# Decoder layer on one core: every engine of the attention stage in the order of emission, softmax in steps of its own, another beginning and end of the stage

## The chip, the cores and the metric

The kernel runs on one core of a Trainium2 chip. The metric is the device time of one execution in microseconds; the figure for the kernel before is the median of three runs. TensorE (PE) multiplies and transposes; VectorE (DVE), ScalarE (ACT) and GpSimd (POOL) work on tiles; SyncE (SP) issues most DMAs. Each engine takes its instructions in a fixed order.

## The reference

One layer, for a prompt of 1024 tokens and 8 sample sequences of 8 new tokens with 4096 cached positions each (64 columns), 1088 columns in all. Cut to what matters:

```python
h = rms_norm(x, norm1) * (1 + scale1) + shift1
z = h @ w_in     # q, kc, vc, ks, vs, kw, vw, gates, conv (bg, cg, h), pool
k_cmp = rms_norm(compress(full[:, :, 0], ...)); v_cmp = compress(full[:, :, 1], ...)
o_cmp, p_cmp = cmp_attention(q, k_cmp, v_cmp, q_pos)
top_i, sel_ok = select_blocks(p_cmp, ...)            # 16 of the 64-token blocks
o_slc = slc_attention(q, top_i, sel_ok, ...)
o_win = window_attention(...)                        # 512 positions back
o_attn = g[..., 0:1] * o_cmp + g[..., 1:2] * o_slc + g[..., 2:3] * o_win
x = x + gate1 * (concat[o_attn, y_conv, y_pool] @ w_out)
x = x + gate2 * swiglu(rms_norm(x, norm2) * (1 + scale2) + shift2, w_up, w_down)
```

There are 8 query heads and 2 key/value heads of 64. The prompt has 16 blocks of 64 tokens, so the selected branch sees every causal block there; for the samples blocks are chosen. The compression makes one key and value of every 32 positions, stride 16, by a small network over the whole cache.

## The kernel before

**Stages.** Normalisation and the input projection run until about 374 us of the span, attention from there to about 832 us, then the output projection and the SwiGLU network. Data are held with features on partitions.

**Who sets the order.** The class `Kernel` emits instructions from tasks, which are generators with a priority (`spawn`, `run`): a task yields the time from which it can go on, and the run takes the task with the lowest priority number that is ready within `MARGIN` (1.2 us). For that the class keeps a clock per engine, `self.t`, advanced by `use` with a cost for each instruction and by `mm` and `tr` for PE. `hold` keeps a task until a condition is true. The emitted instructions then pass through the framework's scheduler, which orders each engine's instructions by its own model of their time; `issue_after(x)` forces that an instruction stands behind x. `together` uses it so that the matmuls of a group follow each other.

**Prompt attention.** 32 units: 8 blocks of 128 queries (`j`), two halves of the heads (`half`), and for each the selected branch with the compressed one (`slc`) and the window branch (`win`). `scores` (from L1015) treats two head pairs (`hl`): three matmuls for each product, since keys and queries are split in a high and a low part (`kh`, `kl`, `qh`, `ql`), into banks of PSUM; the mask with the running maximum on DVE (L1068) reads a bank and frees it; exp with a sum on ACT (L1080); reciprocal and gate on DVE (L1082, L1086); the scale on POOL (L1090). All that is emitted by `scores` itself, pair after pair, into one tile `P` for four heads and 1024 keys, of which there are two. `values` (from L1095) transposes `P` on PE (L143), evacuates it to `pt` (L161, L163), multiplies with the values and stores to `mix_d` in DRAM.

**Samples.** `sample_select` attends to the compressed keys of two sequences and chooses blocks (`kvc`, `qb`, `kn`); 36 sample units follow, nine for each pair of sequences: scores of cached keys (`unit,qb`), mask on DVE (L1325, L1328), exp on ACT (L1332), transposes of `e`, matmuls with the values (`unit,spt`). After the ninth `sample_combine` (from L1360) forms the weights `cw` on ACT and sums twelve parts with `co` on DVE (L1382), transposes it, copies it to `smo` and stores it to `mix_d`.

**Compression.** `compress` works through octets of pages: 16 matmuls each of a `stream` tile (three buffers) with weights. `gather` loads a tile page by page, six pages from SP and two from POOL (L531).

**The edges.** The projection's tiles end with `q0` to `q3`; `head_norm` (L766, L767) normalises each. Then `key_stacks` and `query_parts` split keys and queries, `constants3` (L289 to L342) and `sample_setup` make what the samples need. At the end `output_projection` loads `w_raw` from SP, splits it in `w_hi` and `w_lo`, loads `mixc` from `mix_d` (L1468: the first half of the columns from SP, the second from ACT) and `x1a` (L1494, from ACT), and multiplies `mh`, the high part of `mixc`.

The waits that gate a unit are these:

```python
yield from self.hold(lambda: self.v_done >= u - 1)                                        # prompt_attention
yield from self.hold(lambda: "at" in st and u in self.loads and self.u_done >= u - 1)     # sample_attention
```

Of the kernel before, what the change touches and what calls it, by code (L numbers as in the profile page):

```python
# [17 lines left out]
P = 128  # L18
D = 1024
KT = D // P  # L20
SEQ = 1024
# [40 lines left out]

class Kernel:
    def __init__(self, ctx, tc, ins, outs):
        self.ctx, self.tc, self.nc, self.i, self.o = ctx, tc, tc.nc, ins, outs
        self.ps_ctx = None
        self.t = {"pe": 0.0, "act": 0.0, "dve": 0.0, "pool": 0.0, "dma": 0.0}
        self.table = None
        self.tasks = []
# [56 lines left out]
    def mm(self, out, lhsT, rhs, start, stop, chain=False):  # L126
# [12 lines left out]
        return self.nc.tensor.matmul(out, lhsT, rhs, start=start, stop=stop, skip_group_check=chain)  # L139

    def tr(self, out, in_, ident=None):
        self.t["pe"] += 0.11 if ident is None else 0.03
        return self.nc.tensor.transpose(out, in_, self.ident if ident is None else ident)  # L143

    def together(self, steps):

        last = steps[0]()
        for f in steps[1:]:
            with self.tc.issue_after(last.ins):
                last = f()  # L150
# [442 lines left out]
    def compress_prompt(self, pool):  # L593
# [19 lines left out]
        for kv in range(2):  # L613
            for k in range(KT):
                self.mm(uv[:, kv, 0:P], self.w1[:, kv * KT + k, :], rv[:, kv, k], k == 0, k == KT - 1)
        r = self.compress_evac(uv[:, :, 0:P], vt, pre, 0, 8)
# [269 lines left out]
    def input_projection(self, h):  # L886
# [12 lines left out]
        order = ["kc", "vc", "cg0", "ch0", "bg0", "cg1", "ch1", "bg1", "p0", "ks", "p1", "kw", "q0", "q1", "q2", "q3"]  # L899
        self.ada2 = self.pool("ada2", "left")  # L900
        self.ada_pool = self.ada2.__enter__()
        with self.pool("z", "left") as z, self.pool("hn") as hn:
# [36 lines left out]
            self.spawn(lambda: 0.9 if self.octets <= PACE * (self.z_steps - z0) else 1.5, self.compress_more())  # L939
            with self.pool("conv") as cv:  # L940
                for j in range(2):
                    st = dict(zip(("cg", "ch", "bg"), self.conv_steps(cv, j)))
                    yield from tiles([n + str(j) for n in ("cg", "ch", "bg")],
                                     lambda nm, ch, acc, c0, n: st[nm[:2]](ch, acc))
# [7 lines left out]
            with self.pool("pre") as pp:  # L952
                self.spawn(0.6, self.up_weights_ahead(pp, 1))
                yield from tiles(["q0", "q1", "q2", "q3"], qk)
                yield from self.hold(lambda: self.formed == 2)
            yield from self.hold(lambda: self.prompt_at and self.heads == 18 and 5 in self.ada_at)
# [30 lines left out]
    def key_stacks(self):  # L987

        nc = self.nc
        for j in range(2):  # L990
            kh, kl = self.K[j]
            for a, n, src in ((64, SEQ, self.ksw[:, j, 0:SEQ]), (0, 64, self.kcp)):
                self.split(kh[:, a:a + n], kl[:, a:a + n], src, n)
                yield max(self.t["dve"], self.t["act"]) - 1.0
        self.stacks_at = max(self.t["dve"], self.t["act"])


    def prompt_attention(self, pool):
# [3 lines left out]
        for u, (j, half, br) in enumerate(units):  # L1002
# [3 lines left out]
            yield from self.hold(lambda: self.v_done >= u - 1)  # L1006
# [8 lines left out]
    def scores(self, pool, u, j, half, br):  # L1015
# [31 lines left out]
        Pt = pool.tile([P, 4, SEQ], F32, name="P", bufs=2)  # L1047
        ready = 0.0
        K = self.K[kj]
        for hl in range(2):  # L1050
            r = 2 * half + hl
            st = pool.tile([P, 2, 2, 4], F32, name="st", bufs=6)
            t = [0.0, 0.0]
            for x, (pieces, parts) in enumerate(banks):
# [9 lines left out]
                for g in range(2):  # L1064
                    t[g] = self.t["pe"] + 0.1
                    for (y, col, p0, n, mk) in parts:
                        z = x if y == 0 else 0
                        nc.vector.tensor_tensor_reduce(out=Pt[:, 2 * g + hl, col:col + n], in0=S[g][:, p0:p0 + n], in1=mk,  # L1068
                                                       scale=-1.0, scalar=3e38, op0=OP.add, op1=OP.min,
                                                       accum_out=st[:, g, y, z:z + 1])  # L1070
                        t[g] = self.use("dve", 0.07 + n * 0.00105, t[g])
# [4 lines left out]
            for y, (b, col, n) in enumerate(seg):  # L1076
                sy = st[:, :, y]
                for g in range(2):
                    Ps = Pt[:, 2 * g + hl, col:col + n]
                    nc.scalar.activation(Ps, Ps, AF.Exp, scale=-1.0, bias=sy[:, g, 0:1], accum_out=sy[:, g, 1:2])  # L1080
# [1190 lines left out]
```

## Time and profile before

| | |
|---|---|
| three runs | 1677.99, 1681.29, 1681.86 us, median 1681.29 us |
| the profiled execution | 1672.63 us, span 1671.0 us, mean granted clock 0.977 |
| instructions | 35661 |
| PE busy in the span | 1562.1 us (93%) |
| DVE, ACT, POOL busy | 1090.4, 779.0, 665.4 us |

Times in the trace are counted from the span's start. A row of a timeline gives start, duration, engine, line, operation, output and inputs, shape, how many such instructions stand together, and in square brackets the engine's idle time before and what released it. Lines are those of the kernel before. A wait belongs to the instruction that waited; one that waits for several things is put down to the one that came last. The profiled execution is 8.7 us shorter than the median of the three others.

### The profile page before, as it was taken

The numbers are of one execution on the slowest core, as the hardware profiler recorded it, in microseconds if no ns is written. First come the engines' busy times: TensorE is split into PE (matmuls) and PEld (weight loads), VectorE is DVE, ScalarE is ACT, GpSimd is POOL, SyncE is SP. The second block draws the span as 40 slices with busy tenths as digits, with TensorE's granted clock in tenths as the row PEclk, the third lists the DMA queues.
The fourth block names the chain that finished last, engine by engine and source line by source line (L and its number), as shares of the span: only waits on it lengthen the run. The fifth ranks groups of instructions, "written<-read, shape, count | busy, mean of one in ns | idle before, by whom it ended". The sixth has DMA issues, their size and how long they took to land. (4 is left out here: it accounts for less than half of the span.)

```text
span 1671.0 us, 35661 instructions
## 1 busy us (share of the span) xinstructions
PE 1562.1 (93%) x12697; PEld 1391.8 (83%) x12697; DVE 1090.4 (65%) x2625; ACT 779.0 (47%) x1829; POOL 665.4 (40%) x789
## 2 busy tenths in 40 slices
PE   6899999997999899899599989999999999899998
PEld 2898997896777566566499989999999999899988
DVE  4723234777555666767579878777777775577695
ACT  3522115335765666666466534433434443344462
POOL 3120110114333123223013356554555455788695
PEclk9999999998999999999899999999999999999999
DMA  9585654425467363245685564446444335966553
GB/s 336 182 287 162 207 168 148 144 95 162 133 186 217 100 193 104 70 131 147 210 303 187 198 221 168 143 145 232 145 145 143 142 136 204 393 234 241 182 168 121
DMA packets 186834, 302.12 MB, mean 181 GB/s; under 512 B 26353, under 2 KB 114994, under 8 KB 186338
## 3 DMA queue, kind: packets, MB, share of 16 engines
q1 hardware_dynamic: 166786, 272.20, 49.1%
q0 software_dynamic: 5856, 16.24, 3.0%
q10 hardware_dynamic: 14016, 11.41, 2.2%
q8 instruction: 101, 1.65, 0.4%
q14 instruction: 75, 0.61, 0.1%
HBM read 233.43 MB, written 70.53 MB: 182 GB/s over the span
## 5 line engine op out<-in xcount | busy, mean ns | idle before, releaser
L139 PE MATMUL bank<-b_hi,w_hi 128*128 128x272 f32 x1232 | 351.8, 291 | 7.3 <-DVE f_g L1631 2.9
L139 PE MATMUL bank<-b_lo,w_hi 128*128 128x272 f32 x1232 | 353.8, 289 | 1.7 <-DVE b_lo L171 1.7
L139 PE MATMUL bank<-b_hi,w_lo 128*128 128x272 f32 x1232 | 348.9, 288 | 0.7 <-DVE w_lo L171 0.7
L139 PEld LDWEIGHTS bank<-b_hi,w_hi 128*128 128x128 f32 x1232 | 231.0, 189 | 10.6 <-ACT b_hi L175 4.7
L139 PEld LDWEIGHTS bank<-b_lo,w_hi 128*128 128x128 f32 x1232 | 232.8, 189 | 2.4 <-DVE b_lo L171 2.3
L139 PEld LDWEIGHTS bank<-b_hi,w_lo 128*128 128x128 f32 x1232 | 231.0, 189 | 0.9 <-DVE w_lo L171 0.9
L1090 POOL TENSOR_SCALAR P<-P,st 128x128 f32<-128x128 f32 (+10 forms) x192 | 109.5, 584 | 230.2 <-DVE st L1086 139.1
L171 POOL TENSOR_TENSOR w_s<-w_raw 128x512 f32<-128x512 f32 (+1 forms) x88 | 126.7, 1440 | 64.6 <-DVE w_lo L171 50.5
L171 DVE TENSOR_TENSOR w_lo<-w_raw,w_hi 128x512 fp32r<-128x512 f32 (+2 forms) x121 | 116.9, 975 | 53.8 <-ACT w_hi L175 50.7
L139 PEld LDWEIGHTS bank<-stream 128*128 128x128 f32 x1056 | 127.4, 198 | 17.9 <-issue 13.0
L175 ACT ACTIVATE w_hi<-w_raw 128x512 fp32r<-128x512 f32 (+2 forms) x122 | 80.9, 678 | 130.1 <-PE bank L139 78.2
L171 POOL TENSOR_TENSOR x<-x,d_m 128x272 f32<-128x272 f32 x144 | 126.6, 901 | 34.9 <-DVE x L1833 20.5
L139 PE MATMUL bank<-stream 128*128 128x128 f32 x1056 | 133.8, 284 | 6.2 <-DMA stream<-in_cacheA 5.7
L1080 ACT ACTIVATE P<-P,st 128x640 f32<-128x640 f32 (+12 forms) x192 | 112.7, 588 | 46.1 <-DVE st L1074 26.6
L139 PE MATMUL bank<-h_hi,w_hi 128*128 128x384 f32 (+1 forms) x384 | 130.1, 339 | 0.9 <-ACT py L879 0.6
L139 PE MATMUL bank<-g,w_hi 128*128 128x272 f32 x616 | 121.5, 293 | 8.3 <-DVE x L1833 6.5
L139 PE MATMUL bank<-h_hi,w_lo 128*128 128x384 f32 (+1 forms) x384 | 126.5, 330 | 0.0
L171 DVE TENSOR_TENSOR w_lo<-w_s,w_hi 128x512 fp32r<-128x512 f32 (+1 forms) x124 | 116.8, 944 | 14.8 <-ACT w_hi L175 12.6
L139 PE MATMUL bank<-h_lo,w_hi 128*128 128x384 f32 (+1 forms) x384 | 125.8, 328 | 0.0
L139 PE MATMUL bank<-g,d_hi 128*128 128x272 f32 x616 | 120.2, 291 | 2.6 <-DVE x L1833 1.7
L1833 DVE SCALAR_TENSOR_TENSOR x<-bank,mod,x 128x272 f32<-128x272 f32 (+1 forms) x192 | 87.3, 476 | 40.8 <-PE bank L139 35.5
L139 PEld LDWEIGHTS bank<-g,w_hi 128*128 128x128 f32 x616 | 98.2, 191 | 10.1 <-DVE x L1833 7.4
(371 smaller groups left out, 3732.3 us busy)
## 6 DMA issues: line engine op xcount, KB each, us to landing
g_d<-f_s SPq DMA_DIRECT2D x57, 544.0 KB, 3.3
g<-g_d SPq DMA_DIRECT2D x56, 544.0 KB, 6.3
wada<-in_wada SPq DMA_DIRECT2D x96, 256.0 KB, 5.4
stream<-in_cacheA SPq DMA_DIRECT2D x192, 128.0 KB, 3.2
w_raw<-in_wup SPq DMA_DIRECT2D x40, 512.0 KB, 4.5
unit<-in_cacheB SPq DMA_DIRECT2D x152, 128.0 KB, 2.4
stream<-in_cacheB SPq DMA_DIRECT2D x104, 128.0 KB, 2.4
w_raw<-in_wout SPq DMA_DIRECT2D x24, 512.0 KB, 4.6
```

The source lines that it names most:

```text
L139: return self.nc.tensor.matmul(out, lhsT, rhs, start=start, stop=stop, skip_group_check=chain)
L171: (self.nc.vector if eng == "dve" else self.nc.gpsimd).tensor_tensor(out, a, b, op=op)
L175: self.nc.scalar.activation(hi, src, AF.Copy)
L1080: nc.scalar.activation(Ps, Ps, AF.Exp, scale=-1.0, bias=sy[:, g, 0:1], accum_out=sy[:, g, 1:2])
L1090: nc.gpsimd.tensor_scalar(Ps, Ps, sy[:, g, 3:4], 0.0, op0=OP.mult, op1=OP.add)
L1833: nc.vector.scalar_tensor_tensor(out[:, :n], acc[:, :n], self.mod[:, 5, m, 0:1], out[:, :n], op0=OP.mult, op1=OP.add)
```

## The change

It touches the attention stage and its two edges. The matmuls of the layer stay the same.

- **Order of emission.** In attention each PE instruction is issued behind the PE instruction emitted before it (`in_turn`), and VectorE, ScalarE and GpSimd are reached through a wrapper, `InTurn`, that does the same for each of them, DMAs issued by ScalarE and GpSimd included. SP is not in turn. `together` only calls its steps. The class's costs are replaced by durations that were measured, and a change between half and full rows of the PE array costs 0.08 us on its clock.
- **Softmax.** `scores` emits matmuls and masks only; the exps are one step of a new task `softmax`, the reciprocals, gates and scales another. The samples' exp is a task too, `sample_exp`.
- **Buffers.** `P` holds two heads and has three buffers; the window branch has its own `Pw`, three of 704 columns. A head pair waits for `v_done >= u - 2 + hl`. A sample unit waits for `u_done >= u - 2`, with three `e` and `spt`.
- **Beginning.** The tiles of the projection come in another order, with `bg1` of the convolution last. One octet more is loaded early. The exp table is loaded after the last square root by a small exp. Keys and queries are split in pieces, what the first unit needs first. `constants3` and `sample_setup` come after the first unit's scores.
- **End.** `sample_combine` starts at the exp of the ninth unit, adds ten terms, and the last one when its part is there. The store of `smo` and the loads of `mixc` and `x1a` for the first half of the columns go from POOL.

```diff
+class InTurn:
+    def __getattr__(self, name):
...
+        def call(*args, **kwargs):
+            with self.tc.issue_after(self.last.ins) if self.last else ExitStack():
+                r = f(*args, **kwargs)
+            if hasattr(r, "ins"):
+                self.last = r
+            return r
...
+    def in_turn(self, half, f):
...
+        last, was = self.turn
+        if half != was:
+            self.t["pe"] += 0.08
+        with self.tc.issue_after(last.ins):
+            last = f()
+        self.turn = last, half
+        return last
...
-        order = ["kc", "vc", "cg0", "ch0", "bg0", "cg1", "ch1", "bg1", "p0", "ks", "p1", "kw", "q0", "q1", "q2", "q3"]
+        order = ["kc", "vc", "cg0", "ch0", "bg0", "p0", "ks", "p1", "kw", "q0", "q1", "cg1", "ch1", "q2", "q3", "bg1"]
...
+    def key_stacks(self, ap):
+        self.key_parts(0, 64, P)
+        self.key_parts(0, 0, 64)
+        self.query_parts(ap, 0)
+        self.key_parts(1, 64, P)
+        for j in range(2):
+            self.key_parts(j, 64 + P, SEQ - P)
+        self.key_parts(1, 0, 64)
...
-            yield from self.hold(lambda: self.v_done >= u - 1)
...
-        Pt = pool.tile([P, 4, SEQ], F32, name="P", bufs=2)
+        slc = br == "slc"
         for hl in range(2):
+            yield from self.hold(lambda: self.v_done >= u - 2 + hl)
+            Pt.append(pool.tile([P, 2, SEQ if slc else 5 * P + 64], F32, name="P" if slc else "Pw", bufs=3))
...
-                        t[g] = self.use("dve", 0.07 + n * 0.00105, t[g])
+                        t[g] = self.use("dve", 0.16 + n * 0.00105, t[g])
...
+            self.spawn(-1, self.softmax(j, r, st, Pt[hl], seg, max(t), done))
...
+    def softmax(self, j, r, st, Ps_, seg, t, done):
+        yield t - MARGIN
...
+                nc.scalar.activation(Ps, Ps, AF.Exp, scale=-1.0, bias=sy[:, g, 0:1], accum_out=sy[:, g, 1:2])
+                ta = self.use("act", 0.28 + n * 0.00084, t + 0.1, table="exp")
+        yield ta + 0.1 - MARGIN
...
+                nc.gpsimd.tensor_scalar(Ps, Ps, sy[:, g, 3:4], 0.0, op0=OP.mult, op1=OP.add)
+                at = self.use("pool", 0.25 + n * 0.00084, td + 0.1)
+        done.append(at + 0.1)
...
-            yield from self.hold(lambda: "at" in st and u in self.loads and self.u_done >= u - 1)
+            yield from self.hold(lambda: "at" in st and u in self.loads and self.u_done >= u - 2)
...
+        if nx == 9:
+            self.spawn(2, self.sample_combine(pool, st, u // 9))
...
-        for c in range(11):
+        for c in (0, 1, 2, 3, 4, 5, 6, 7, 8, 10):
             nc.vector.scalar_tensor_tensor(o, part[:, c], w[:, c:c + 1], o, op0=OP.mult, op1=OP.add)
-        yield self.use("dve", 4.0, self.t["pe"]) + 0.5
+        yield self.use("dve", 3.7, self.t["pe"])
+        yield from self.hold(lambda: "last" in st)
+        nc.vector.scalar_tensor_tensor(o, part[:, 9], w[:, 9:10], o, op0=OP.mult, op1=OP.add)
...
-        nc.sync.dma_start(self.mix_d[:, 0:4, SEQ + 16 * p:SEQ + 16 * p + 16],
-                            mo.rearrange("p r b t -> p r (b t)"))
+        nc.gpsimd.dma_start(self.mix_d[:, 0:4, SEQ + 16 * p:SEQ + 16 * p + 16], mo.rearrange("p r b t -> p r (b t)"))
...
+        with self.tc.issue_after(self.last_sqrt.ins):
+            self.nc.scalar.activation(self.warm, self.eps, AF.Exp)
...
+        yield from self.hold(lambda: self.scored >= 1)
+        self.constants3(ap)
+        self.sample_setup(ap)
...
-                (nc.sync if c == 0 else nc.scalar).dma_start(t, self.mix_d[:, k:k + 2, c * HALF:c * HALF + HALF])
+                (nc.gpsimd if c == 0 else nc.scalar).dma_start(t, self.mix_d[:, k:k + 2, c * HALF:c * HALF + HALF])
...
-                nc.scalar.dma_start(dst, src)
+                (nc.gpsimd if c == 0 else nc.scalar).dma_start(dst, src)
```

Counted in the two orders, PE changes between tile shapes in attention 323 times before and 276 times now, and between half and full rows 233 and 195 times.

In the following rows a name's number tells instances of one tile apart; in the changed kernel the instructions of DVE, ACT and POOL in attention all have the wrapper's line, L78, a matmul has L164 and a transpose L169. The first place is the start of attention on PE, before, from the sums of squares of the last query tiles (`h_sq`) on:

```order
L139 MATMUL bank<-h_sq,mean_h 128x384
L139 MATMUL bank<-h_sq,mean_h 128x320
L139 MATMUL bank<-stream 128x128 x16
L139 MATMUL bank<-kh_3506,qh 128x192 x2
L139 MATMUL bank<-kl_3507,qh 128x192 x2
L139 MATMUL bank<-kh_3506,ql 128x192 x2
...
L139 MATMUL bank<-kh_3508,ql 128x128 x2
L139 MATMUL bank<-stream 128x128 x32
L143 MATMUL bank<-ident,P 128x64 x8
```

One octet stood ahead of the first scores and two behind all of them. The same place now, from the last matmul of the projection (`h_hi`, of the tile bg1) on:

```order
L164 MATMUL bank<-h_hi_102,w_lo 128x320
L164 MATMUL bank<-stream 128x128 x32
L164 MATMUL bank<-kh_3538,qh 128x192 x2
...
L164 MATMUL bank<-kh_3540,ql 128x128 x2
L164 MATMUL bank<-stream 128x128 x16
L164 MATMUL bank<-kh_3540,qh 128x128 x2
L164 MATMUL bank<-kl_3541,qh 128x128 x2
L164 MATMUL bank<-kh_3540,ql 128x128 x2
L164 MATMUL bank<-stream 128x128 x16
```

Two octets stand ahead of the scores, and one more behind each head pair of the window. On DVE, before, the two last query norms and the constants of the samples stood ahead of the first masks:

```order
L171 TENSOR_TENSOR ql<-q,qh 128x512 x2
L766 RECIPROCAL h_sq<-h_sq 128x384
L766 RECIPROCAL h_sq<-h_sq 128x320
L767 SCALAR_TENSOR_TENSOR q<-bank,qgain_s,h_sq 128x384
L767 SCALAR_TENSOR_TENSOR q<-bank,qgain_s,h_sq 128x320
L289 TENSOR_SCALAR t_3699<-ti 128x1
L297 TENSOR_SCALAR d_3705<-di 128x128
```

And now, from the masks' casts to the first masked scores:

```order
L78 CAST m_cmp<-m 128x8
L78 TENSOR_TENSOR kl_3539<-kv__93,kh_3538 128x128
L78 TENSOR_TENSOR kl_3539<-kcp,kh_3538 128x64
L78 TENSOR_TENSOR ql<-q,qh 128x512
L78 TENSOR_TENSOR kl_3541<-kv__93,kh_3540 128x128
L78 TENSOR_TENSOR kl_3539<-kv__93,kh_3538 128x896
L78 TENSOR_TENSOR kl_3541<-kv__93,kh_3540 128x896
L78 TENSOR_TENSOR kl_3541<-kcp,kh_3540 128x64
L78 COPY kn<-kv__93 128x128
L78 MEMSET pre 128x2
L78 COPY pre<-bank 64x128 x4
L78 ISA P,st<-bank,m_slc 128x128
```

The norms are done, the constants are gone from here, and the copies of an octet's result (`pre`) stand ahead of the first mask. The second place is the middle, on PE, before: the scores of a selected unit and of the window unit, then the transposes of the selected unit's `P`:

```order
L139 MATMUL bank<-kh_3508,qh 128x512 x2
L139 MATMUL bank<-kl_3509,qh 128x512 x2
L139 MATMUL bank<-kh_3508,ql 128x512 x2
L139 MATMUL bank<-unit,qb 64x512 x2
L139 MATMUL bank<-kh_3508,qh 128x512 x2
L139 MATMUL bank<-kl_3509,qh 128x512 x2
L139 MATMUL bank<-kh_3508,ql 128x512 x2
L139 MATMUL bank<-vt,c_w_82 64x256 x2
L143 MATMUL bank<-ident,P 128x64 x32
```

The two window pairs follow each other there. The same part of the program now:

```order
L169 MATMUL bank<-ident,Pw 128x64 x32
L164 MATMUL bank<-unit,qb 64x512 x2
L164 MATMUL bank<-kh_3540,qh 128x512 x2
L164 MATMUL bank<-kl_3541,qh 128x512 x2
L164 MATMUL bank<-kh_3540,ql 128x512 x2
L169 MATMUL bank<-ident,e 128x128 x4
L164 MATMUL bank<-pt,vt__286 64x256 x8
L164 MATMUL bank<-kh_3540,qh 128x512 x2
...
L164 MATMUL bank<-kh_3538,qh 128x384 x2
...
L169 MATMUL bank<-ident,P 128x64 x32
```

The transposes of an earlier window unit (`Pw`), sample work and value matmuls stand between the two pairs, and the next unit's first pair (128x384) stands ahead of the transposes of `P`. The third place is the end, on POOL now:

```order
L78 TENSOR_SCALAR Pw<-Pw,st 128x640 x2
L78 TENSOR_SCALAR Pw<-Pw,st 128x63 x2
L78 DMA mix_d<-smo 128x4x16
L1553 DMA mixc<-mix_d 128x2x272 x4
L1579 DMA x1a_10598<-in_xT 128x2x272 x4
L208 TENSOR_TENSOR w_lo<-w_raw,w_hi 128x512
```

The store of `smo` and the loads of `mixc` stand behind each other as they did on SP before, and the loads of `x1a` follow them.

More of the change, by code (lines that the diff above doesn't have):

```diff
@@ L60, with __init__ @@
 }
+class InTurn:
+    def __init__(self, tc, of, names=()):
+        self.tc, self.of, self.last = tc, of, None
+        for name in names:
+            setattr(self, name, InTurn(tc, getattr(of, name)))
+    def __getattr__(self, name):
+        f = getattr(self.of, name)
+        if not callable(f):
+            return f
+        def call(*args, **kwargs):
[4 more added lines that the diff above has]
+            return r
+        return call
 class Kernel:
@@ L138, in mm @@
         self.t["pe"] += cost
-        return self.nc.tensor.matmul(out, lhsT, rhs, start=start, stop=stop, skip_group_check=chain)
+        return self.in_turn(lhsT.shape[0] <= 64,
+                            lambda: self.nc.tensor.matmul(out, lhsT, rhs, start=start, stop=stop, skip_group_check=chain))
     def tr(self, out, in_, ident=None):
         self.t["pe"] += 0.11 if ident is None else 0.03
-        return self.nc.tensor.transpose(out, in_, self.ident if ident is None else ident)
+        ident = self.ident if ident is None else ident
+        return self.in_turn(ident.shape[0] <= 64, lambda: self.nc.tensor.transpose(out, in_, ident))
+    def in_turn(self, half, f):
+        if self.turn is None:
+            self.last_pe = f()
+            return self.last_pe
+        last, was = self.turn
[5 more added lines that the diff above has]
+        return last
     def together(self, steps):
[L147 to L150, printed above, removed]
+        for f in steps:
+            f()
     def mm3(self, out, a, b, start, stop, chain=False):
@@ L1098, in values @@
+    def values(self, pool, u, j, half, br, Pt, seg, done):
         nc = self.nc
@@ L1108, in values @@
                     tiles.append((col + t * P, P, [self.vt[:, kt, vo + 64 * g:vo + 64 * g + 64] for g in range(2)]))
-        yield ready
+        yield from self.hold(lambda: len(done) == 2)
+        yield done[1]
         yield from self.hold(lambda: self.v_done == u)
@@ L1188, in sample_select @@
         kv = []
-        yield from self.hold(lambda: self.cmp_done >= 2 * p + 2)
+        yield from self.hold(lambda: self.cmp_done >= 2 * p + 2 and self.selected == p)
         for b2 in range(2):
```

128 lines of the change are left out of this document (74 added, 54 removed).

## The prediction

> **What bounds the kernel now.** I began with the head of the page, for the busiest engine, and then took the attention stretch (374 to 832 us of the span) by windows, because every moved instruction lies there or at its two edges. The columns of the windows are start:end, length, busy time and count of each engine, the granted TensorE clock, the DMA share and GB/s.
>
> ```profile
> span 1671.0 us, 35661 instructions
> PE 1562.1 (93%) x12697; PEld 1391.8 (83%) x12697; DVE 1090.4 (65%) x2625; ACT 779.0 (47%) x1829; POOL 665.4 (40%) x789
> ...
> 374.00:400.00 26.00, 16.60 (x120) 15.28 (x119) 18.40 (x76) 10.09 (x34) 13.60 (x38) 0.74 0.49 141
> ...
> 550.00:600.00 50.00, 41.65 (x396) 28.32 (x397) 30.47 (x130) 30.15 (x76) 12.14 (x21) 0.90 0.40 123
> ...
> 800.00:832.00 32.00, 16.59 (x168) 10.82 (x167) 16.09 (x46) 13.33 (x33) 0.00 (x0) 0.84 0.63 207
> sum 458.00, PE 404.36 PEld 286.17 DVE 291.37 ACT 284.17 POOL 139.78; mean PE 40.44 PEld 28.62 DVE 29.14 ACT 28.42 POOL 13.98
> ```
>
> PE is busy for 93% of the span. In attention it is busy for 404.4 of 458.0 us, so 53.6 us are idle; no other engine there is busy for more than 64%. 9.4 us of the idle lie in the first window and 15.4 us in the last, so some 29 us are spread over the 400 us between. What PE waits for there, from the waits view (total us, times, longest):
>
> ```profile
> PE bank L143 <- POOL P L1090: 11.4, 5, 3.1
> PE bank L139 <- DVE st L1068: 9.0, 6, 3.7
> PE bank L139 <- ACT mh L175: 7.9, 1, 7.9
> PE bank L143 <- DVE co L1382: 6.9, 1, 6.9
> PE bank L139 <- DVE q L767: 5.2, 1, 5.2
> ```
>
> None of these is a shortage of throughput. They are moments at which the next row of PE's fixed order isn't ready. A second loss doesn't count as idle: the clock was granted at half speed in seven stretches (their windows, first, fourth and last, and the sum of all):
>
> ```profile
> 381.50:395.20 13.70, 6.24 (x35) 5.97 (x36) 11.76 (x63) 5.28 (x24) 3.11 (x9) 0.50 0.70 203
> ...
> 572.70:576.10 3.40, 2.95 (x37) 2.83 (x38) 3.26 (x13) 3.18 (x8) 1.74 (x3) 0.50 0.00 0
> ...
> 821.80:835.50 13.70, 4.33 (x18) 4.04 (x19) 5.02 (x13) 4.37 (x11) 0.00 (x0) 0.50 0.94 312
> sum 47.80, PE 30.04 PEld 22.29 DVE 34.45 ACT 27.79 POOL 11.33; mean PE 4.29 PEld 3.18 DVE 4.92 ACT 3.97 POOL 1.62
> ```
>
> Work done at half speed takes twice its time, so half of the 30.0 busy us, 15.0, were lost: 3.1 at the start, 2.2 at the end, 9.7 in the five stretches between.
>
> **The beginning.** The timeline of PE, and of DVE and SP beside it:
>
> ```profile
> 375.08 3.73 PE L139 MATMUL bank<-stream 128*128 128x128 f32 x32
> 379.79 0.35 PE L139 MATMUL bank<-kh,ql 64*128 64x192 f32 x2 [0.58 <-DVE ql L171]
> 385.30 0.53 PE L139 MATMUL bank<-kh,qh 64*128 64x192 f32 x2 [5.16 <-DVE q L767]
> 390.07 0.44 PE L139 MATMUL bank<-kh,qh 64*128 64x128 f32 x1 [3.66 <-DVE st L1068]
> 391.51 9.14 PE L139 MATMUL bank<-stream 128*128 128x128 f32 x64
> ...
> 380.26 4.55 DVE L766 RECIPROCAL h_sq<-h_sq 128x384 f32<-128x384 f32 x2
> ...
> 378.84 2.94 SPq L531 DMA_DIRECT2D stream<-in_cacheA  x6
> ```
>
> One octet of the compression is 32 records, 3.7 us. Before, one octet covers the wait for kl and ql, the last two reciprocals of the query norm (4.55 us) stand bare, and constants3 stands ahead of the first masks (3.66 us); two octets come after the scores, mostly at half clock. Now the last projection tile is bg1, whose 72 matmuls cover the norm of q3, and two octets (7.4 us) stand ahead of the first scores. Ahead of kl and ql DVE has only the casts, 128 columns of keys and half of the query: about 5 us, an estimate from the same instructions on DVE before, less than 7.4. A third octet and a fourth follow between the score rows; the fourth needs a refilled buffer (an issue of 2.94 us and a landing of 3.2, below), and some 10 us lie between the first octet's end and it. So the 9.4 us of idle and 3.1 of half clock can go. Against it constants3 (its DVE work) now stands between the first masks and the first reciprocals, and can hold the transposes about a microsecond. Term: -11, ends -12.5 and -3 (if constants3 or the pre copies cost PE what the masks' wait and the bare norm cost now).
>
> **The middle.** Before, PE runs the four head scores of a unit in one piece and then asks for its P:
>
> ```profile
> 573.15 1.97 PE L143 MATMUL bank<-ident,P 64*128 64x64 f32 x32 [3.15 <-POOL P L1090]
> ...
> 585.74 0.38 PE L139 MATMUL bank<-kh,qh 64*128 64x320 f32 x1 [2.75 <-DVE st L1068]
> ...
> 566.62 0.59 POOL L1090 TENSOR_SCALAR P<-P,st 128x31 f32<-128x31 f32 x2 [19.04 <-DVE st L1086]
> ...
> 569.89 4.55 POOL L1090 TENSOR_SCALAR P<-P,st 128x512 f32<-128x512 f32 x6 [0.77 <-DVE cs L1369]
> ```
>
> POOL had been idle for 19 us, then had all the scales at once, and PE waited 3.15 us for them. In the new order pairs of heads alternate with window transposes, sample work and an octet, and the next unit's first pair of heads stands ahead of this unit's transposes; P of two heads in three buffers allows it. The instructions are the same, so only waits go. P waits from 11.4 to about 3 (-8), the waits for masks, without the 3.66 of the beginning, from 5.3 to about 3 (-2), the others -1: term -11, ends -22 (three quarters of the 29) and 0 (the waits come back at other rows).
>
> The half clock of the middle follows gaps. The stretch at 572.7 begins within the 3.15 us gap; I let half of the 9.7 us go: -5, ends -9.7 and 0. [...]
>
> **Switches of shape.** A matmul of another tile shape starts later behind its forerunner:
>
> ```profile
> 789.96 0.31 PE L139 MATMUL bank<-kh,ql 64*128 64x320 f32 x2
> 790.11 0.30 PE L139 MATMUL bank<-kh,qh 64*128 64x320 f32 x1
> 790.35 1.08 PE L139 MATMUL bank<-pt,vt__286 128*64 128x256 f32 x8
> ```
>
> 0.15 us to the same shape, 0.24 to the other: 0.09 each. Counted in the two orders, such switches in attention fall from 323 to 276: 47 x 0.09 = -4 (ends -3 and -5).
>
> **The end.** The last attention matmul ends at 816.4; then PE waits twice:
>
> ```profile
> 823.27 0.47 PE L143 MATMUL bank<-ident,co 128*128 128x128 f32 x1 [6.88 <-DVE co L1382]
> ...
> 831.64 1.50 PE L139 MATMUL bank<-mh,w_hi 128*128 128x272 f32 x5 [7.89 <-ACT mh L175]
> ...
> 814.66 1.90 DVE L1382 SCALAR_TENSOR_TENSOR co<-part,cw,co 128x128 f32<-128x128 f32 x5
> 822.87 0.35 DVE L1382 SCALAR_TENSOR_TENSOR co<-part,cw,co 128x128 f32<-128x128 f32 x1
> ...
> 826.52 2.05 SPq L1468 DMA_DIRECT2D mixc<-mix_d  x4
> 831.16 0.43 ACT L175 ACTIVATE mh<-mixc 128x272 fp32r<-128x272 f32 x1 [6.19 <-DMA mixc<-mix_d]
> ```
>
> Eleven terms of 0.35 us are under 4 us, yet they last from 814.66 to 823.2, since seven w_lo of the output projection stand among them. In the new order the w_lo still stand there, ten terms come earlier by program but the weights cw are now behind evacuations on ACT, which sets the chain back some 3 us, and only its last term needs the last unit. The loads of mixc still stand behind the store of smo, now on POOL's queue instead of SP's. So neither wait goes: term +2, ends -3 and +4. The medians from issue to landing on the two queues, for the same transfer:
>
> ```profile
> stream<-in_cacheA SPq DMA_DIRECT2D x192, 128.0 KB, 3.2
> ...
> stream<-in_cacheA POOLq DMA_DIRECT2D x64, 128.0 KB, 3.3
> ```
>
> The queue costs 0.1 us by that; it is no term. [...]
>
> **What the fixed order itself costs.** An engine that takes its work in order of emission stops at the first instruction that isn't ready, with everything behind it. DVE holds masks that free PSUM banks, ACT holds exps and evacuations, POOL holds page loads and stores besides the scales:
>
> ```profile
> L1090 POOL TENSOR_SCALAR P<-P,st 128x128 f32<-128x128 f32 (+10 forms) x192 | 109.5, 584 | 230.2 <-DVE st L1086 139.1 <-ACT pt L161 28.0 <-ACT P L1080 19.5
> L531 POOL DMA_DIRECT2D stream<-in_cacheA x36 | 20.1, 558 | 32.2 <-PE bank L139 13.7 <-DMA unit<-in_cacheB 6.2 <-DMA stream<-in_cacheA 4.7
> ```
>
> Before, the order was fixed too once built, but by other costs. No row prices the difference. The lower end is 0; the upper end is 28: as if the 28 us for which scales waited for evacuations fell on PE. I take +7, a quarter, because all three engines are idle for a third of the stretch or more.
>
> Cover: the reordered projection ahead of 374 us and the work behind 835 us have the same instructions. In the last 94 us of the projection PE's longest wait is this:
>
> ```profile
> PE bank L139 <- ACT py L879: 1.5, 1, 1.5
> ```
>
> The stores, norms and weights that are moved there lie under PE's matmuls; without that cover two such waits would be 3 us. I put 0 for both parts, ends -3 and +3.
>
> **Sum:** -11 - 11 - 5 - 4 + 2 + 7 = -22 us. The profiled execution took 1672.6 us, 8.7 under the median of the runs (1681.3), so the median should be 1681.3 - 22 = 1659.
>
> **Rivals.** (1) *Nothing measurable*: the waits of the middle move to other rows (0 for its idle and its clock) and the fixed order costs about 11; -11 - 4 + 2 + 11 = -2, 1679. For it: the waits are short and many, and any order has its own. Against: POOL's pile at 566 to 574 has a cause in the order, which is taken away.
>
> (2) *Slower*: the page loads on POOL. 36 issues, two to an octet, are 18 stops; five of them waited for PE to free a buffer, 13.7 us, 2.7 each. If scales are caught behind each of the 18, and the transposes behind these, PE loses 18 x 2.7 = 49 us instead of the 7 in my sum: -22 + 42 = +20, 1701. It decides from 29 / 18 = 1.6 us per octet upwards. Against: POOL is busy for 31% of the stretch, and scales are wanted a pair of heads later than they are made.
>
> (3) *More*: the middle loses 22 of its 29 idle us and all 9.7 of half clock, and the fixed order costs 2 us: -11 - 22 - 9.7 - 4 + 2 + 2 = -43, 1638.
>
> (4) *The clock doesn't answer to short gaps*: the five half-speed stretches of the middle stay, whatever is filled: -22 + 5 = -17, 1664. It lies within the forecast. For it speaks that the stretch at 419 us has only a gap of 0.9 us ahead; against it the one at 572.7. [...]
>
> **Chances.** Forecast, from -33 to -8 us: 0.58, with (4) 0.3 of it. (3), further down: 0.16. (1): 0.10. (2), any cost above +5: 0.16. A measurement of this kernel tells 0.3%, 5 us, from no change. Faster 0.58 + 0.16 = 0.74, same 0.10, slower 0.16. Range: down to 1634, just past (3), up to 1687, through (1) and the mild half of (2), leaving out 0.06 below and 0.11 above. The forecast's own range is 1648 to 1673.
>
> **What would show it.** Beginning: no wait for q or ql above 1 us, and the first transposes of P some 19 us after the last projection matmul instead of 26. Middle: PE idle between 400 and 800 us under 20 us and its waits for P near 3; fewer windows at 0.5. Fixed order: the idle ahead of POOL's page loads and DVE's masks, and whether PE waits right after. End: two waits near 7 us each again. I am wrong if PE's idle time in attention stays near 54 us: then order was not what it waited for, but throughput at the softmax; or if PE's busy time rises, which an equal count of matmuls only allows through the clock.

## The result and the profile after

The change made the kernel slower: 1705.5 us (median of four runs) against 1679.9, ratio 1.0147, 95% interval 1.0126 to 1.0168. Forecast was 1659, range 1634 to 1687.

The profile of the changed kernel by stages (projection, attention to its last matmul, the way to the first output matmul, the rest), after the head of its page; the columns are those of the windows in the prediction:

```profile
span 1699.2 us, 35607 instructions
...
0.00:383.30 383.30, 353.49 (x2345) 308.94 (x2345) 180.93 (x291) 124.30 (x230) 58.33 (x90) 0.97 0.59 187
383.30:840.40 457.10, 404.30 (x4031) 287.37 (x4031) 285.83 (x1204) 269.64 (x747) 140.44 (x259) 0.93 0.46 138
840.40:860.60 20.20, 0.50 (x3) 0.18 (x1) 10.59 (x31) 5.88 (x12) 6.46 (x9) 0.60 0.78 260
860.60:1699.20 838.60, 812.20 (x6320) 803.88 (x6320) 621.11 (x1114) 371.84 (x834) 460.17 (x444) 0.98 0.56 193
```

The kernel before was profiled a second time (run e8 below), because its first profile was the shortest of all its executions. The same four stages there:

```profile
0.00:375.90 375.90, 350.37 (x2342) 306.71 (x2343) 175.68 (x288) 121.44 (x223) 58.77 (x91) 0.98 0.59 192
375.90:827.40 451.50, 413.18 (x4035) 292.81 (x4034) 283.39 (x1207) 279.08 (x763) 139.55 (x255) 0.93 0.47 141
827.40:843.50 16.10, 0.53 (x2) 0.24 (x2) 7.82 (x19) 5.08 (x12) 0.00 (x0) 0.63 0.80 258
843.50:1683.80 840.30, 812.25 (x6320) 803.99 (x6320) 621.84 (x1114) 373.74 (x834) 465.12 (x444) 0.98 0.56 193
```

Against this profile the projection is 7.4 us longer, attention 5.6, the way to the output 4.1, the rest 1.7 shorter: 15.4 together, of the 25.6 between the medians. The changed kernel's profile is its fastest execution and the second one of before took 1685.4 us, 5.5 above the median; where the other 10 us lie, these profiles don't show.

PE's time in attention splits in idle time (length less busy), what half speed lost (estimated as half of the busy time in the half-speed stretches) and the rest, which I call work. By the first profile of before that is rather too much: 32 transposes of `P` took 1.22 us at a granted clock of 1.00 (at 755.19) and 1.97 us at 0.50 (at 573.15), eight `pt` matmuls 1.08 us (at 578.94) and 1.97 us (at 683.04), 1.6 and 1.8 times as long. The sums over the half-speed stretches of attention, twelve in the changed kernel and nine in the second profile of before:

```profile
sum 65.10, PE 57.24 PEld 39.67 DVE 43.24 ACT 36.22 POOL 14.39; mean PE 4.77 PEld 3.31 DVE 3.60 ACT 3.02 POOL 1.20
```

```profile
sum 61.50, PE 50.34 PEld 36.87 DVE 43.80 ACT 41.31 POOL 25.38; mean PE 5.59 PEld 4.10 DVE 4.87 ACT 4.59 POOL 2.82
```

| attention, us | length | idle | lost to half speed | work |
|---|---|---|---|---|
| before, first profile | 442.5 | 38.9 | 12.9 | 390.7 |
| before, second profile | 451.5 | 38.3 | 25.2 | 388.0 |
| changed | 457.1 | 52.8 | 28.6 | 375.7 |

So by this estimate PE's work fell by 12 to 15 us (by 11 with 1.6 times instead of twice), and the changed kernel gave as much back in waiting (14 us) and lost more time at half speed. What it waits for, from the waits of PE between 370 and 860 us:

```profile
PE bank L164 <- ACT qh L78: 21.0, 7, 5.3
PE bank L169 <- DVE co L78: 11.4, 1, 11.4
PE bank L164 <- ACT mh L212: 9.7, 2, 8.3
PE bank L164 <- DVE pt L78: 6.3, 5, 2.7
PE bank L169 <- ACT pt L78: 3.5, 2, 2.8
PE bank L164 <- ACT vt L78: 3.2, 1, 3.2
PE bank L169 <- POOL Pw L78: 2.3, 1, 2.3
...
PE bank L169 <- POOL P L78: 1.4, 2, 0.9
...
PE bank L164 <- DVE st L78: 0.7, 2, 0.5
```

The waits that I had wanted gone are gone: P by POOL 11.4 before and under 4 now (`P` and `Pw`), masks 9.0 and 0.7. In their place stands one that the kernel before has not at all: seven waits for `qh`, one at each new block of queries. The timeline of ACT and PE at the first of them:

```profile
417.64 0.38 ACT L78 ACTIVATE pt<-bank 128x256 f32<-128x256 f32 x1 [4.35 <-PE bank L169]
419.00 1.28 ACT L78 ACT_TABLE_LOAD   x1 [0.97 <-DVE kvo L78]
...
423.08 0.56 ACT L78 ACTIVATE vt<-bank 64x128 f32<-64x128 f32 x2 [2.31 <-PE bank L164]
...
426.06 1.28 ACT L78 ACT_TABLE_LOAD   x1 [0.48 <-ACT mo L78]
...
428.71 0.61 ACT L78 ACTIVATE qh<-q 128x512 fp32r<-128x512 f32 x1
...
429.38 0.63 PE L164 MATMUL bank<-kh,qh 64*128 64x320 f32 x2 [5.27 <-ACT qh L78]
```

`query_parts` is emitted together with the scores that need it. Before, the scheduler moved the split ahead: the second block's `qh` started at 377.0 and its first matmul at 416.0. Now they start at 428.7 and 429.4. In turn on ACT the split stands behind an octet's evacuation (`vt`), two table loads of 1.28 us, a copy (`mo`) and four exps.

### The profile page after: what moved, and what is told of

Same layout as the page of the kernel before. It is cut to its first block, busy times and chain, and to the rows that moved or that the text cites. A ratio compares the mean times of both kernels' runs of the same rounds, so it can differ in the third digit from the quotient of the medians.

```text
span 1699.2 us, 35607 instructions
## 1 busy us (share of the span) xinstructions
PE 1570.5 (92%) x12697; PEld 1400.4 (82%) x12697; DVE 1098.5 (65%) x2638; ACT 771.7 (45%) x1821; POOL 665.4 (39%) x801
## 4 chain that ended last, share of the span: by engine, by line
PE 69%; DVE 12%; DMA 6%; ACT 5%; issue 4%; POOL 2%; SPq 1%; ACTq 0%; DVEq 0%; POOLq 0%
PE bank L164 66%; PE bank L169 3%; DVE w_lo L208 2%; DMA stream<-in_cacheA 1%; DVE x L1918 1%; DVE P L78 1%; SPq L568 1%; DMA w_raw<-in_wup 1%; DMA x1b<-in_xT 1%; ACT Pw L78 1%; DMA wada<-in_wada 1%; ACT P L78 1%; POOL w_s L208 1%; DVE d_lo L208 1%; DVE pt L78 1%
## 5 line engine op out<-in xcount | busy, mean ns | idle before, releaser
L164 PE MATMUL bank<-b_lo,w_hi 128*128 128x272 f32 x1232 | 355.3, 290 | 2.5 <-DVE b_lo L208 2.5
L164 PE MATMUL bank<-b_hi,w_hi 128*128 128x272 f32 x1232 | 352.1, 291 | 5.3 <-DVE f_g L1716 2.9
L164 PE MATMUL bank<-b_hi,w_lo 128*128 128x272 f32 x1232 | 350.3, 290 | 1.2 <-DVE w_lo L208 1.2
L164 PEld LDWEIGHTS bank<-b_hi,w_hi 128*128 128x128 f32 x1232 | 231.8, 190 | 8.1 <-ACT b_hi L212 3.9
L164 PEld LDWEIGHTS bank<-b_lo,w_hi 128*128 128x128 f32 x1232 | 234.1, 190 | 3.4 <-DVE b_lo L208 3.4
L164 PEld LDWEIGHTS bank<-b_hi,w_lo 128*128 128x128 f32 x1232 | 232.3, 190 | 1.4 <-DVE w_lo L208 1.4
L164 PEld LDWEIGHTS bank<-stream 128*128 128x128 f32 x1056 | 131.9, 205 | 18.9 <-issue 10.5
L164 PE MATMUL bank<-stream 128*128 128x128 f32 x1056 | 137.6, 291 | 10.0 <-DMA stream<-in_cacheA 6.5
L208 POOL TENSOR_TENSOR x<-x,d_m 128x272 f32<-128x272 f32 x144 | 124.6, 885 | 36.5 <-DVE x L1918 20.2
L164 PE MATMUL bank<-h_hi,w_hi 128*128 128x384 f32 (+1 forms) x384 | 129.8, 338 | 0.0
L164 PE MATMUL bank<-g,w_hi 128*128 128x272 f32 x616 | 122.1, 294 | 6.6 <-DVE x L1918 5.4
L164 PE MATMUL bank<-h_hi,w_lo 128*128 128x384 f32 (+1 forms) x384 | 127.7, 333 | 0.0
L164 PE MATMUL bank<-h_lo,w_hi 128*128 128x384 f32 (+1 forms) x384 | 126.5, 329 | 0.0
L208 DVE TENSOR_TENSOR w_lo<-w_s,w_hi 128x512 fp32r<-128x512 f32 (+1 forms) x124 | 115.3, 933 | 15.6 <-ACT w_hi L212 13.4
L164 PE MATMUL bank<-g,d_hi 128*128 128x272 f32 x616 | 119.2, 290 | 4.5 <-DVE x L1918 2.3
L164 PEld LDWEIGHTS bank<-g,w_hi 128*128 128x128 f32 x616 | 98.7, 192 | 8.4 <-DVE x L1918 6.0
L1746 POOL TENSOR_TENSOR f_g<-f_g,f_v 128x272 f32<-128x272 f32 x44 | 44.0, 999 | 152.1 <-DVE f_v L1716 131.0
L78 POOL TENSOR_SCALAR P<-P,st 128x128 f32<-128x128 f32 (+14 forms) x120 | 63.7, 547 | 101.3 <-DVE st L78 91.8
```

Source lines behind the costliest of these rows:

```text
L78: r = f(*args, **kwargs)
L164: lambda: self.nc.tensor.matmul(out, lhsT, rhs, start=start, stop=stop, skip_group_check=chain))
L208: (self.nc.vector if eng == "dve" else self.nc.gpsimd).tensor_tensor(out, a, b, op=op)
L1746: nc.gpsimd.tensor_tensor(g[:, 1], s1, v, op=OP.mult)
```

## The experiments

Theories at the start: (1) the late query split is the loss; (2) the fixed order as such is; (3) the edges are. All times below are medians, in us; the kernel before was run beside each group and had 1679 to 1681.

**e1, the query split half a block earlier.**

```diff
-            if half == 0 and br == "slc":
-                if j:
-                    self.query_parts(self.query_pool, j)
+            if br == "slc":
+                if half == 0 and j:
+                    self.qs = self.next_qs
+                if half == 1 and j < 7:
+                    now = self.qs
+                    self.query_parts(self.query_pool, j + 1)
+                    self.next_qs, self.qs = self.qs, now
```

> The changed kernel, but the split of the next block's queries (qh on ACT, ql on DVE) is emitted half a block earlier, at the second half's first unit; all engines stay in turn. Theory 1 (the split is emitted at the moment of need and in a fixed order nothing can move it ahead): the seven waits of 21.0 us for qh go, and with them a part of the half-speed stretches, 1705 falls to about 1675 (1668 to 1686). Theory 2 (the fixed order as such costs, whatever stands first): the waits turn up at the next rows, 1695 to 1705. Theory 3 (the loss lies at the edges, the projection's order and the end): 1703 or more.

Measured: 1707.1. Theory 1 falls in this form. PE's waits are now these:

```profile
PE bank L169 <- DVE st L78: 15.7, 7, 6.0
PE bank L169 <- DVE co L78: 11.8, 2, 11.3
PE bank L169 <- ACT e L78: 6.8, 5, 3.6
...
PE bank L169 <- POOL P L78: 5.9, 4, 3.3
```

The waits for `qh` are gone, others of the same size stand at the transposes, and idle time in attention is 57 us. PE's work is 384 us here, though PE is still in order; why it rises isn't known.

**e2 to e4, which engines are in turn.**

```diff
-        self.nc = InTurn(self.tc, nc, ("vector", "scalar", "gpsimd"))
+        self.nc = InTurn(self.tc, nc, ("vector", "gpsimd", ))      # e2; e3 and e4: self.nc = nc
...
-        self.turn = self.last_pe, False                            # e4 alone, with the chain in together
```

> The changed kernel with ACT's order left to the scheduler; PE, DVE and POOL stay in turn. Theory 1: the scheduler moves qh ahead again, about 1680, PE's waits for qh under 5 us. Theory 2: ACT is one of four fixed orders, so a quarter to a half of the loss: 1690 to 1700. Theory 3: 1703.

> The changed kernel with only PE in order of emission; DVE, ACT and POOL left to the scheduler. Theory 1: like the kernel with ACT free or a little better, 1672 to 1682. Theory 2, if the order of the three other engines is what costs: also 1672 to 1682; if PE's own order is what costs: 1695 or more. Theory 3: 1700.

> The changed kernel without any order of emission (no engine in turn, the groups chained as in the kernel before); the softmax steps, buffers, projection order and end stay. Theory 1: about the time before, 1675 to 1685, since qh moves ahead. Theory 2: the same or below, 1670 to 1685. Theory 3: the edges stay, so 1695 or more.

Measured: ACT free 1705.9, PE alone in turn 1689.9 (ratio to before 1.0063, 1.0042 to 1.0083), no engine in turn 1695.8 (1.0091, 1.0067 to 1.0114). So the order of DVE, ACT and POOL costs 15.6 us, and PE's order brings 5.9. That is theory 2, and not for ACT alone: with ACT free, PE waits for `ql` on DVE instead (17.4 us in seven waits). In attention:

| attention, us | length | idle | lost to half speed | work |
|---|---|---|---|---|
| PE alone in turn (e3) | 442.0 | 46.4 | 16.8 | 378.8 |
| no engine in turn (e4) | 452.9 | 35.7 | 20.6 | 396.6 |

PE's order saves work and costs waits. In these profiles the order of the three others adds 6 us of idle time and 12 at half speed; the last section shows how much the latter varies. e3 lies between the theories. And e2 and e4 came out as theory 3 had said: 1695.8 without any order is still 16 above before, and its projection ends at 385.6, some 10 us later. So the edges count too.

**e5 and e17, DVE free, POOL free.** Theory 4: DVE is the engine that counts; 5: POOL with its page loads, the prediction's second rival; 6: waits pass from engine to engine.

> The changed kernel with DVE's order left to the scheduler; PE, ACT and POOL stay in turn. Theory 4 (DVE is the engine that counts: masks and evacuations stand behind copies and reciprocals that wait for ACT): about 1690, as with DVE, ACT and POOL all free. Theory 5 (POOL with its page loads): 1705. Theory 6 (the waits pass from engine to engine, and freeing one helps little): 1698 to 1706.

> The changed kernel with POOL's order left to the scheduler; PE, DVE and ACT stay in turn. Theory 5 (POOL's page loads and stores hold the scales up, the rival of the prediction): 1690 to 1697. Theories 6 and 7: freeing one engine whose neighbours keep their order brings nothing, as with ACT (1705.9) and DVE (1713.9) free: 1702 to 1712.

Measured: 1713.9 and 1710.9. Freeing one of three neighbours doesn't help; theories 4 and 5 fall. Both programs have more half speed in attention (busy 68 and 75 us in such stretches, against 57; the mean granted clock is 0.959 in both profiles, against 0.962), and with POOL free idle time there is 52.6 us, as in the changed kernel. POOL does stop at its page loads in the changed kernel:

```profile
POOL stream L78 <- PE bank L164: 39.0, 9, 13.6
```

but PE waits for POOL only the 3.7 us above.

**e6, the projection's tiles in the old order.**

```diff
-        order = ["kc", "vc", "cg0", "ch0", "bg0", "p0", "ks", "p1", "kw", "q0", "q1", "cg1", "ch1", "q2", "q3", "bg1"]
+        order = ["kc", "vc", "cg0", "ch0", "bg0", "cg1", "ch1", "bg1", "p0", "ks", "p1", "kw", "q0", "q1", "q2", "q3"]
```

> The changed kernel with the projection's tiles in the order of the kernel before (both convolutions first, q3 last); all else stays. In the profile of the changed kernel the projection ended 9.4 us later, with equal work, and in the four variants 10 to 15 us later. If the tiles' order does it: the projection ends near 374 to 379 again; but attention's first wait for the norm of q3 (5.2 us) comes back in part, so 1697 to 1703. If it is the varying clock of single executions: the projection ends at 383 and the time is 1705 or, with the wait for the norm, 1710.

Measured: 1697.3 (1.0103, 1.0082 to 1.0123): 8.2 us less, the projection ends at 377.0. It ends at 383 to 389 in each of the eleven profiles with the new order of tiles, and at 374 to 377 in each of the eight with the old one. In the changed order PE has new waits there, none of which the kernel before has in either profile:

```profile
PE bank L164 <- ACT stream L198: 2.9, 2, 2.3
PE bank L164 <- ACT ko L681: 1.6, 1, 1.6
PE bank L164 <- ACT vt L661: 1.5, 1, 1.5
```

I followed one of them: at the wait for `vt` (215.0), the compression's `pre` had stood on DVE behind the pooling's `pe_x`. For the others the cause isn't shown.

**e7 and e10, the end.** e7 keeps the first `w_lo` behind the copies of `smo` on DVE; e10 puts the end of before back.

```diff
-        (self.nc.vector if eng == "dve" else self.nc.gpsimd).tensor_tensor(out, a, b, op=op)
+        late = eng == "dve" and self.behind_n > 0
+        self.behind_n -= late
+        with self.tc.issue_after(self.behind.ins) if late else ExitStack():
+            (self.nc.vector if eng == "dve" else self.nc.gpsimd).tensor_tensor(out, a, b, op=op)
```

> The changed kernel, but the first w_lo of the output projection are issued on DVE behind the copies of smo, so the chain of co runs through. The chain lasted from 841.4 to 851.7 with eight w_lo in it, 6.3 us of its own work being near 4. If these splits, which wait for their weights, set the end: the first output matmul comes 6 to 7 us earlier, 1698. If the loads of the weights or of mixc set it: 1704 to 1706, with the wait moved to mh.

> The changed kernel with the end of the kernel before (sample_combine after the ninth unit's values, eleven terms in one go, smo and the first mixc from SP, x1a from ACT); all else stays. The end took 20.2 us in the changed kernel against 15.2 and 16.1 in the two profiles of the kernel before. If these edits cost it: 1700 to 1702. If the weight loads that now come with the last matmul, instead of 8 us earlier, set it: 1704 to 1707.

Measured: 1714.3 and 1709.4, both above the times expected. In e7 the wait for `co` halves and the one for `mh` grows:

```profile
PE bank L165 <- ACT mh L216: 14.9, 2, 12.3
...
PE bank L170 <- DVE co L78: 5.6, 1, 5.6
```

so the chain wasn't what set the end, which is 18.4 us instead of 20.2; and the rest of the kernel is 8.5 us longer. In e10 the end is 20.4 us, as in the changed kernel. So the edits of the end cost nothing by this run; that the weight loads, which now start with the last matmul, cost the 4 us is what remains, not shown.

**e8, the kernel before once more.**

> The kernel before, unchanged, profiled a second time, to see how much its stages vary. If the first profile (1672.6) was a lucky one: the projection ends some 5 us later than 373.9 and the clock is a little lower; if single executions are alike: within 2 us at each stage's end.

Measured: 1685.4, its stages above. The projection ends 2.0 us later than in the first profile; idle time and work in attention are nearly the same, the loss to half speed is not: see the last section.

**e9, a clock with measured costs.** Theory 7: a fixed order is as good as the clock that makes it. The change had corrected masks, exps and scales; the evacuations and the step of reciprocal and gate it had left too small.

```diff
-        if max(self.t["act"], r) + 0.06 + n * 0.00083 <= max(self.t["dve"], r) + 0.07 + n * 0.00104:
+        ca, cd = (0.17 + n * 0.00083, 0.15 + n * 0.00104) if self.turn else (0.06 + n * 0.00083, 0.07 + n * 0.00104)
+        if max(self.t["act"], r) + ca <= max(self.t["dve"], r) + cd:
...
-            td = self.use("dve", 0.16, ta + 0.1)
+            td = self.use("dve", 0.34, ta + 0.1)
```

The trace of the changed kernel for these instructions (count, busy, mean ns, idle before):

```profile
L78 ACT ACTIVATE pt<-bank 128x512 f32<-128x512 f32 x54 | 29.8, 593 | 19.9 <-PE bank L169 16.7 <-issue 2.5 <-DVE st L78 0.5
...
L78 DVE COPY pt<-bank 128x512 f32<-128x512 f32 x58 | 37.4, 684 | 21.6 <-PE bank L169 20.3 <-issue 1.0
...
L78 DVE TENSOR_TENSOR st<-st,gates 128x2 f32<-128x2 f32 x96 | 17.2, 179 | 3.3
L78 DVE RECIPROCAL st<-st 128x2 f32<-128x2 f32 x96 | 15.4, 160 | 2.4 <-ACT Pw L78 1.1 <-ACT P L78 1.1
```

> The changed kernel with the clock's undersized costs in attention set to what its trace shows: an evacuation on ACT 0.17 + 0.00083n and on DVE 0.15 + 0.00104n (128x512 took 0.59 and 0.68 us, the clock had 0.48 and 0.60), reciprocal and gate 0.34 instead of 0.16. Theory 7 (a fixed order is as good as its clock, and these gaps make the waits): PE's idle time in attention falls from 53 to 35 or less, 1685 to 1693. Theory 6 (waits pass from engine to engine in any fixed order of four engines): 1700 to 1708.

Measured: 1692.3 (1.0080, 1.0056 to 1.0104), 13.2 less by nothing but the numbers from which the order is made (and, for an evacuation, the choice between ACT and DVE). Idle time in attention falls less than theory 7 said, to 45.8, and the waits for `qh` stay (19.8 us, seven).

**e13 to e15, the repairs together.** e13 is e9 with the early query split, e14 that with the old order of tiles, e15 that with two more costs corrected.

> The changed kernel with the corrected costs and the query split emitted half a block earlier. With the costs alone 1692.3 was measured, and PE still waited 19.8 us for qh; with the early split alone the waits moved to other rows and nothing was gained. Theory 7b (the early split could bring nothing as long as the clock misplaced everything else): its waits now go for good, 1672 to 1682. Theory 6b (they move again, as they did): 1688 to 1696.

> The same with the projection's tiles in the order of before. The tiles alone brought 8.2 us in the changed kernel. Theory 7b: 1665 to 1674, faster than the kernel before. Theory 6b: 1680 to 1688. If the gain of the tiles' order hangs on the rest: as e13.

> The same as e14 with two more costs corrected: the evacuation of an octet (four copies on ACT of 0.27, four on DVE of 0.29 us, which wait for each other; the clock had 0.7 and 0.8), and the copy and the store of mo on ACT. Theory 7 (the order is as good as its clock): some 5 us less than e14. Theory 6b: no difference beyond 4 us.

Measured: 1686.5, 1678.3 and 1687.8. The early split, worth nothing alone, takes 5.8 off once the clock is right, less than theory 7b said. In attention of e13

```profile
386.40:827.20 440.80, 401.08 (x4031) 286.67 (x4031) 292.24 (x1221) 266.94 (x740) 141.47 (x259) 0.94 0.49 147
```

39.7 us are idle, as many as before, and the work is the changed kernel's 375.8: attention is 10.7 us shorter than in the second profile of before. The tiles take another 8.2. With all three e14 stands at 0.9976 of before (0.9954 to 0.9998), between what the two theories had said. But e15, with a truer clock still, is 9.5 us slower than e14: idle time 46.7. So truer costs don't always give a better order, and theory 7 holds for e9 only. What makes the better order better isn't shown.

**e11, PE alone in turn with the old edges; e12, the kernel before with PE in turn; e16, that with the costs.**

```diff
+    def in_turn(self, f):                       # e12, in the kernel before, for mm and tr in attention
+        if self.turn is None:
+            self.last_pe = f()
+            return self.last_pe
+        with self.tc.issue_after(self.turn.ins):
+            self.turn = f()
+        return self.turn
```

> Only PE in order of emission, with the projection's tiles and the end of the kernel before; softmax steps, two-head buffers and the beginning of attention stay. If the three losses add (15.6 for the order of DVE, ACT and POOL, 8.2 for the tiles, some 4 for the end): 1705.5 - 28 = 1677, level with the kernel before or a little faster. If the order on PE alone needs the late convolution tile: 1685.

> The kernel before with one thing of the change: PE in attention in order of emission. PE's work in attention, idle time and half speed taken out, is 376 us in the changed kernel against 391 and 388 before; with PE alone in turn it was 379, with none 397. If PE's order brings that in any surrounding: 12 us less work, and with the same waits 1668; if the kernel before, whose scores hold the softmax with them, then waits at the rows that it now can't pass: 1680 to 1695.

> The kernel before with PE in attention in order of emission (1676.5 alone) and the corrected costs in its clock. Theory 7: the order on PE fits better, idle time in attention falls from 47.6 to 40 or less: 1666 to 1672. If the three free engines' scheduler hides the clock's errors: 1674 to 1679.

Measured: 1698.6, 1676.5 and 1684.6, none of them as expected. The gains didn't add up in e11, which is 8.7 us slower than e3 with the new edges: its projection ends at 375.2, but attention takes 457 us and the rest 853, 13 more than in before. e16 likewise loses behind attention. In e4, e7, e11 and e16 the part from the last attention matmul on takes 860 to 866 us, against 855 and 856 in before, and PE is idle for 32 to 39 us of it behind the first output matmul, against 28 (in e11, 7.7 of it for `w_lo`). Why stays open. e12 beats both kernels, as e14 does, by a quarter of a per cent: 0.9977 of before (0.9966 to 0.9988), from ten runs:

```profile
374.80:822.00 447.20, 399.56 (x4035) 283.86 (x4033) 282.80 (x1204) 279.67 (x762) 139.41 (x255) 0.94 0.48 143
```

47.6 us idle instead of 38, but 379 of work instead of 388 to 391.

## Why the prediction was wrong

- **Failed: what the fixed order itself costs, +7, and with it the middle, -11.** The waits that the middle priced did go; others took their place, and for those I took a quarter of a row of POOL's waits. Measured, the order of DVE, ACT and POOL costs 15.6 us (e3), and idle time in attention rises by 14 where -13 was forecast (beginning -9, middle -11, order +7). Some 8 of the 14 are there with PE alone in turn (46.4 in e3 and 47.6 in e12, 38 to 39 before): PE's own order wasn't priced at all. I had checked the order at three places and priced the waits that would go, not the new waits at the head of each engine's line; the split of the queries stood in ACT's order and I didn't look there. It was the largest wait, but not the cause alone: moved ahead, it only passed the waits on (e1). The range of the term (0 to 28) did hold the cost; its value was taken too low.
- **Failed: cover, 0 for the projection's new order.** It costs 8.2 us (e6), beyond the end of +3. "The same instructions" hid that the same instructions in another order bring PE new waits for ACT there, 6.0 us by the rows above.
- **Undersized: switches, -4.** PE's work fell by 12 to 15 us. No one group of matmuls carries it: in busy time, half speed included, `kh,qh` falls from 52.2 us in the first profile to 46.9, `kl,qh` from 42.9 to 39.8, `kh,ql` from 40.6 to 39.6 and the transposes of `P` from 60.9 to 58.1 (`P` and `Pw`); the octets have 81.1 and 81.9. That switches make all of it isn't shown.
- **Right in the main: the beginning.** The first transposes of `P` come 21.7 us after the projection's last matmul, 26.7 before, with an octet more ahead of them:

```profile
383.88 7.41 PE L164 MATMUL bank<-stream 128*128 128x128 f32 x64 [0.58 <-DVE cy L848]
...
393.86 0.42 PE L164 MATMUL bank<-kh,qh 64*128 64x128 f32 x1 [1.65 <-DVE pre L78]
...
404.98 1.12 PE L169 MATMUL bank<-ident,P 64*128 64x64 f32 x12 [0.48 <-POOL P L78]
```

That is 5.0 and an octet of 3.7, or 8.7 of the 11. Right behind, PE stops 3.2 us for `vt` on ACT, a wait that the term doesn't have.
- **The end: the mechanism right, the size not.** Both waits stayed, the one for `co` longer (11.4 us against 6.9): +4 to +5 where +2 was forecast with an end of +4.
- **The half clock, -5**, didn't come: the loss in attention is 28.6 us against 12.9 and 25.2 in the two profiles of before. Against so wide a spread the size of the rise isn't shown. Of the seven waits for `qh`, five were followed by a stretch at half speed; those at 486.8 (2.06 us) and 647.8 (1.75 us) weren't. Nor does each stretch of the middle before follow a longer gap: in the 5 us ahead of the one at 681.9 none is above 0.51 us. And "twice its time" is too much by the rows above: at 1.6 to 1.8 times, 11 to 14 of the 30.0 busy us were lost before, not 15.0.
- **The rivals.** (2), slower, had the right sign and the wrong engine: page loads on POOL stop POOL for 39 us, and PE waits for POOL 3.7 us; POOL free gains nothing (e17). (1) had the mechanism, waits that move to other rows, and too small a cost.
- **The sign of being wrong.** Idle time didn't fall. But that it would then be throughput at the softmax isn't borne out: the same work with other costs and the early split has 39.7 us of idle time (e13), so the order still decides. And PE's busy time doesn't rise through the clock alone: with an equal count of matmuls its work, the loss to half speed taken out, is 375.7 us in the changed kernel, 384 in e1 and 396.6 in e4.

## What to carry to other kernels

An order of emission forced on several engines hangs on the costs and the moments of emission behind it: costs alone moved this kernel by 13 us down (e9) and, corrected further, 9 up (e15). Look, on each engine that is put in turn, for what is emitted just when it is needed, and see what stands ahead of it there. Force one engine at a time: PE alone gave 3 to 6 us (e12 against before, e3 against e4; with other costs, in e16, nothing), while the three others cost more than that. And when a stage is moved, price its waits as well as its work.

## What the hardware showed

The half-speed stretches vary between executions of one program with the same waits. In attention the kernel before had 38.9 and 38.3 us of idle time in its two profiles, but 25.8 and 50.3 us of PE's busy time at half speed: 12 us of difference by the estimate of half, 9 us at 1.6 times, with nothing else changed. The same transposes of `P`, with the same wait of 2.63 us ahead, in the first and the second profile, and the stretch behind each (the granted clock is the third number from the end):

```profile
755.19 1.22 PE L143 MATMUL bank<-ident,P 64*128 64x64 f32 x32 [2.63 <-POOL P L1090]
...
763.24 1.94 PE L143 MATMUL bank<-ident,P 64*128 64x64 f32 x32 [2.63 <-POOL P L1090]
```

```profile
755.00:765.00 10.00, 9.81 (x136) 7.04 (x138) 7.85 (x32) 7.56 (x22) 4.53 (x9) 1.00 0.37 109
...
763.30:766.70 3.40, 3.40 (x42) 2.95 (x44) 2.11 (x9) 3.40 (x13) 2.70 (x6) 0.50 0.00 0
```

In the changed kernel each of the twelve stretches starts in or behind a gap of 1.6 us or more; two of them, with the gaps ahead:

```profile
609.92 1.59 PE L169 MATMUL bank<-ident,Pw 64*128 64x64 f32 x16 [2.81 <-ACT pt L78]
...
720.32 0.49 PE L164 MATMUL bank<-kh,qh 64*128 64x512 f32 x1 [1.61 <-DVE spt L78]
```

```profile
608.90:615.80 6.90, 5.76 (x36) 3.36 (x36) 5.53 (x23) 3.83 (x11) 1.03 (x2) 0.51 0.70 206
721.60:728.40 6.80, 6.80 (x53) 5.45 (x53) 6.46 (x34) 5.05 (x11) 1.66 (x3) 0.50 0.01 5
```

A gap of 1.61 us was followed by 6.8 us at half speed. What decides whether such a stretch follows a gap, and how long it lasts, isn't shown. So a single profile of this kernel can be an estimated 9 to 12 us off in attention by the clock alone (attention in the two profiles of before took 442.5 and 451.5 us), and stages are better compared by idle time and work than by length.
